# Two decoder blocks on one core: token tiles put in order of precedence at the layer boundaries, boundary weights split on VectorE, recurrence constants computed earlier

## The chip, the cores and the metric

The kernel runs on one core of a Trainium2 chip. The metric is the device time of one execution in microseconds. Engines: TensorE (PE; PEld are its weight loads), VectorE (DVE), ScalarE (ACT), GpSimd (POOL) and SyncE (SP, whose queue issues most DMAs).

## The reference

512 tokens of width 1024 in float32 go through a first block of two layers and then a second block with its own mixers and a feed-forward part. Only what lies around the change is cut out here:

```python
h = _layernorm(x, ln_in_g, ln_in_b)
for layer in range(2):
    proj = jnp.einsum('bsd,de->bse', h, w_in[layer])     # 13 segments: aq ak av ag bq bk bv bf bg cq ck cv cg
    ...                                                  # three attentions, gated: ya, yb, yc
    y = jnp.einsum('bse,ed->bsd', jnp.concatenate([ya, yb, yc], -1), w_out[layer])
    h = _layernorm(sqrt(2) * h + y, ln_g[layer], ln_b[layer])   # DEEPNORM_ALPHA = 4 ** 0.25
# second block
p_lb = softmax(hgrn_lb_logits, axis=0); lower_bounds = cumsum(p_lb, axis=0) - p_lb[0:1]
h = rms_norm(x, attn_norm); proj = h @ w_in              # bi, iw, bf, ... are segments of it
...
log_f = logaddexp(log(max(lb, 1e-30)), log1p(-lb) + log_sigmoid(f_raw)); k_in = (1 - lb) * sigmoid(-f_raw)
```

Every norm works on one token at a time, over its 1024 values.

## The kernel before

**Tiling.** The tokens are four tiles of 128 (NT = 4), one token per partition. A projection needs the normed tokens transposed, features on the partitions, and nearly in full float32 precision: both operands are held as a rounded part (hi) and a residual (lo), and mm3 (lines 193 to 199) makes three matmuls of each product: hi·hi, hi·lo, lo·hi. For the tokens this split is made by split_half (253): four transposes on TensorE into PSUM, a cast to hi on ScalarE (262), the residual on VectorE (263, tile hTl). For the weights it is made by weights (167): a DMA on SP's queue into wraw, a cast on ScalarE (189, whi), a subtraction (190, wlo). The subtraction is VectorE's, except where the caller gives another engine: the weights at the start and at the ends of the two layers (lines 343, 345, 367, 1060, 1061) give GpSimd. There are two buffers of whi and two of wlo.

**A layer's end** (layer1, 555 to 610). most (564) adds six of the eight parts of the output projection to the residual tiles res, in four column blocks c of 256 and in each over the four tiles t; line 576 is the addition on VectorE. Then rest(t) (590) adds the last two parts for a tile: two halves of six matmuls of 512 columns, each added on VectorE with a sum for the mean (598). norm(t) (601) is the layer norm (272): line 276 the mean, 278 a pass on ScalarE for the sum of squares, 279 and rsqrt (217; 221, 241, 245: seven dependent operations on one column), 286 and 287 gain and bias on each half, then a store of the tile on SP's queue (603). After the first layer split_x follows and values' step (347), which projects the tile (two groups of 24 matmuls); after the second the rms norm of the second block (post_rms, 857: squares on ScalarE, rsqrt, scaling in line 847), its transposes, and begin2's step (1063), again two groups of 24.

**The order of the work.** A scheduler fixes the order of every engine when the program is built. An instruction's place is its position in the program, less the offset of an enclosing high_priority; as the engines come free in the builder's reckoning, each takes the ready instruction with the lowest place. HP is 3000. The attention parts run with an offset of HP (ahead, 132). pipe (289) writes the stages for the tiles skewed, stage 0 of tile t beside stage 1 of tile t - 1, without any offset, and rest is called for all four tiles before it:

```python
for t in range(NT):
    rest(t)
self.pipe(*tail)          # tail: norm, the post stages, the next stage's projection
```

**The start** (355). Tile 0 of x is loaded, then the first weights; norm(t) loads the tiles 1 to 3 itself (378). Gain and bias rows are made by 32 small matmuls (373).

**The constants.** Hgrn's constructor (1522), at the start of the second block, computes the lower bounds and their logarithms: two DMAs on ScalarE's queue, eight operations on 1 to 8 columns on VectorE and three activations (1529 to 1543).

Of the kernel before, what the change touches and what calls it, by code (L numbers as in the profile page):

```python
# [13 lines left out]
AF = mybir.ActivationFunctionType  # L14
ALU = mybir.AluOpType
# [4 lines left out]
P = 128  # L20
S = 512
NT = S // P
D = 1024
KD = D // P
# [4 lines left out]
HP = 3000  # L29
# [4 lines left out]
class Net:  # L34
    def __init__(self, ctx, tc, a, out):
        self.ctx, self.tc, self.nc, self.a, self.out = ctx, tc, tc.nc, a, out
        pool = lambda name, bufs=1, **k: ctx.enter_context(tc.tile_pool(name=name, bufs=bufs, **k))
        self.cp = pool("const")
        self.sb = pool("sb")
        self.pool = None  # L40
        self.ps = pool("ps", space=PSUM)
        self.dr = pool("dr", space=DRAM)
        self.n = 0
        self.setup()

    def nm(self, s):
# [117 lines left out]
        self.sel = sel  # L164


    def weights(self, parts, n, kt=KD, eng=None):

        nc = self.nc

        def flat(tag, bufs, dt=F32, k=kt):
            m = 1056 if dt == F32 else 2112
            return self.t(tag, [P, m], bufs, dt)[:, :k * n].rearrange("p (k n) -> p k n", k=k)

        hi, lo = flat("whi", 2, F32R), flat("wlo", 2, F32R)
        kh = kt // 2 if kt % 2 == 0 else kt
        while kh * n > 1056:
            kh = (kh + 1) // 2
        parts = parts if isinstance(parts, list) else [(0, 0, parts)]
        for ka in range(0, kt, kh):  # L180
            kb = min(ka + kh, kt)
            raw = flat("wraw", 3, F32, kb - ka)
            for k0, c0, src in parts:
                k1, nn = k0 + src.shape[0] // P, src.shape[1]
                x, y = max(k0, ka), min(k1, kb)
                if x < y:
                    nc.sync.dma_start(raw[:, x - ka:y - ka, c0:c0 + nn],
                                      src[(x - k0) * P:(y - k0) * P].rearrange("(k p) n -> p k n", p=P))
            nc.scalar.copy(hi[:, ka:kb], raw)  # L189
            (eng or nc.vector).tensor_sub(lo[:, ka:kb], raw, hi[:, ka:kb])  # L190
        return hi, lo

    def mm3(self, out, wh, wl, xh, xl, nk, start=True, stop=True):
# [92 lines left out]
            nc.vector.scalar_tensor_tensor(y, y, mv[:, 2:3], g[half], op0=ALU.add, op1=ALU.mult)  # L286
            nc.vector.scalar_tensor_tensor(y, y, mv[:, 5:6], b[half], op0=ALU.mult, op1=ALU.add)

    @staticmethod
    def pipe(*stages):  # L290

        for t in range(NT + len(stages) - 1):
            for s, f in enumerate(stages):
                if 0 <= t - s < NT:
                    f(t - s)

    def new_hT(self):
        return (self.t("hTh", [P, KD, S], 1, F32R), self.t("hTl", [P, KD, S], 1, F32R))
# [37 lines left out]
    def values(self, l, hT, w=None):  # L336


        nc = self.nc
        v = [self.u("v", [P, D], NT) for _ in range(NT)]  # L340
        lf = self.u("lf", [P, NT, 16], 1)
        self.vl = v, lf
        w = w or self.weights(self.src1(l, "bv", 0, 260), 260, eng=nc.gpsimd)
        if l:
            wc = self.weights(self.src1(l, "cv"), 256, eng=nc.gpsimd)

        def step(t):
            ps = self.proj_n(w, 260, hT, t)
            nc.scalar.copy(v[t][:, 512:768], ps[:, 0:256])
            nc.vector.tensor_add(lf[:, t, 0:4], ps[:, 256:260], self.bfb[:, l, :])  # L350
            if l:
                nc.scalar.copy(v[t][:, 768:1024], self.proj_n(wc, 256, hT, t))
        return step

    def start(self, hT):

        nc, a = self.nc, self.a
        xs = [self.tk() for _ in range(NT)]

        def load(t):  # L360
            nc.sync.dma_start(xs[t], a["x"][0, t * P:(t + 1) * P, :])

        gb = self.tok.tile([16, P], F32, name="gb8", tag="gb8")
        for j, name in enumerate(("ln_in_g", "ln_in_b")):
            nc.scalar.dma_start(gb[8 * j:8 * j + 8], a[name].rearrange("(k n) -> k n", k=8))
        load(0)
        first = self.weights(self.src1(0, "bv", 0, 260), 260, eng=nc.gpsimd)
        self.bfb = self.c("bfb", [P, 2, 4])

        g, b = ([self.p(tag) for tag in tags] for tags in (("s", "s"), ("pv", "s")))  # L370
        for j, r in enumerate((g, b)):
            for k in range(8):
                nc.tensor.matmul(r[k // 4][:, k % 4 * P:k % 4 * P + P], lhsT=self.ident[:16, 8 * j + k:8 * j + k + 1].broadcast_to([16, P]),
                                 rhs=gb, start=True, stop=True)

        def norm(t):
            if t:
                load(t)
            if t == 1:
                nc.sync.dma_start(self.bfb, a["b_forget"].rearrange("(o l) h -> o l h", o=1).broadcast_to([P, 2, 4]))  # L380
            st = self.ln_stats()
            halves = [xs[t][:, :S], xs[t][:, S:]]
            if t:
                for j, x in enumerate(halves):
                    nc.scalar.activation(self.wa([P, S], BF16), x, AF.Identity, accum_out=st[:, j:j + 1])
            else:
                bs = self.tok.tile([P, 2, 6], F32, name="ln_b", tag="ln_b")
                for j, x in enumerate(halves):
                    nc.vector.bn_stats(bs[:, j], x)
                nc.vector.bn_aggr(st[:, 0:2], bs)  # L390
            self.layernorm(xs[t], g, b, 1e-5, st, sums=t > 0)
            nc.gpsimd.dma_start(self.hres[:, t, :], xs[t])

        self.pipe(norm, lambda t: self.split_x(hT, t, xs[t], ("tr", "tr")), self.values(0, hT, first))

    def small1(self, pool):

# [49 lines left out]
    def layer1(self, l, hT, post, nxt):  # L447


        nc, a = self.nc, self.a  # L450
# [71 lines left out]
        scale = 64 ** -0.5  # L522
        rb, rc, ra, rg = RATES[:4]
        with self.tp(f"att{l}", "right") as self.sub:
# [30 lines left out]
            with self.tp(f"bnd{l}", "right") as self.tok:  # L555
# [48 lines left out]

                sts = {}
                tail = [norm] + [lambda t, f=f: f(t, res[t]) for f in post] + [nxt()]
                for t in range(NT):
                    rest(t)
                self.pipe(*tail)
                left.close()  # L610

    def out_tokens(self, W, xh, xl, order, evac):
# [59 lines left out]
    def att_b(self, bq, bk, v, lf, out, slot):  # L672
# [6 lines left out]
        nc.scalar.activation(e, e, AF.Ln, bias=1.0)  # L679
        nc.vector.scalar_tensor_tensor(x, x, 0.0, e, op0=ALU.min, op1=ALU.subtract)  # L680
        nc.vector.tensor_copy(lf[:, :, 4:8], x)
        nc.vector.tensor_copy(lf[:, :, 8:16], lf[:, :, 0:8])
        cumr = self.wa()
        nc.gpsimd.memset(cumr, 1.0)
# [365 lines left out]
    def begin2(self, hT):  # L1050

        self.ph1.close()
        self.phase = self.ctx2.enter_context(self.tp("ph2", "left"))
        self.ph2i = self.ctx2.enter_context(ExitStack())
        pool = self.ph2i.enter_context(self.tp("ph2i", "left"))
        self.nslot, self.na, self.npw = 24, 4, 3
        self.bi = pool.tile([P, NT, S], F32, name="bi", tag="bi")
        self.iw = self.u("iw", [P, NT, 8], 1)
        pool = self.nc.gpsimd
        ws = [self.weights(self.col2("bi", 0, 256), 256, eng=pool),  # L1060
              self.weights([(0, 0, self.col2("bi", 256, 256)), (0, 256, self.col2("iw", 0, 8))], 264, eng=pool)]

        def step(t):
            self.nc.scalar.copy(self.bi[:, t, 0:256], self.proj_n(ws[0], 256, hT, t))
            ps = self.proj_n(ws[1], 264, hT, t)
            self.nc.scalar.copy(self.bi[:, t, 256:512], ps[:, :256])
            self.nc.scalar.mul(self.iw[:, t, :], ps[:, 256:264], (64 ** -0.5) * (8 ** -0.5))
        return step
# [450 lines left out]
class Hgrn:  # L1519


    def __init__(self, net, hT, col):
        self.net, self.nc, self.hT, self.col = net, net.nc, hT, col
        nc, a = net.nc, net.a
        s = lambda tag, n: net.u(tag, [P, n], 1)

        lg, e, den, lb, la, l1, kc, gb = (s(t, n) for t, n in (("hlg", 4), ("hle", 4), ("hld", 4), ("hlb", 4),
                                                                ("hla", 4), ("hl1", 4), ("hkc", 8), ("hgb", 1)))
        nc.scalar.dma_start(lg, a["hgrn_lb_logits_2"][0].rearrange("(h p) -> p h", p=P))
        nc.vector.tensor_sub(e, lg, lg)  # L1530
        nc.scalar.activation(e, e, AF.Exp)
        nc.vector.reciprocal(den, e)
        nc.vector.tensor_mul(e, e, den)
        nc.vector.tensor_sub(lb, e, e)
        nc.vector.tensor_scalar_max(la, lb, 1e-30)
        nc.scalar.activation(la, la, AF.Ln)
        nc.scalar.activation(l1, lb, AF.Ln, scale=-1.0, bias=1.0)
        nc.vector.tensor_scalar(kc[:, 0:4], lb, -0.5, 0.5, op0=ALU.mult, op1=ALU.add)
        nc.vector.tensor_scalar(kc[:, 4:8], lb, 0.5, -0.5, op0=ALU.mult, op1=ALU.add)
        nc.scalar.dma_start(gb, a["hgrn_out_norm_2"][0].rearrange("(p o) -> p o", o=1))  # L1540

        nc.vector.tensor_scalar_mul(gb, gb, 0.25)
        self.la, self.l1, self.kc, self.gb = la, l1, kc, gb
        self.lev = net.sub.tile([P, 9, P], F32R, name="lev", tag="lev")
        nc.gpsimd.dma_start(self.lev, a["c_lev"])
        self.lmask = net.sub.tile([P, 8, P], BF16, name="lmask", tag="lmask")
# [231 lines left out]
```

## Time and profile before

| | |
|---|---|
| median of 3 runs | 1684.64 us (1684.13 to 1685.22) |
| the profiled execution | 1684.35 us, its span 1682.6 us |
| TensorE busy | 1619.7 us (96%), 9320 matmuls |
| VectorE busy | 1067.2 us (63%), 2355 instructions |
| ScalarE busy | 730.1 us (43%), 1484 instructions |
| GpSimd busy | 129.2 us (8%), 139 instructions |

The span runs from the first to the last instruction of one execution; the time has a little around it. Busy shares are means over the span. A timeline row gives the start and the duration in us, the engine, the line of the program, the operation, what it writes and reads, its shape, and in brackets how long the engine stood idle before it and which instruction ended that. Matmuls overlap, so their spacing and not their duration is what one costs.

### The profile page before, as it was taken

How to read it: one execution, taken by the hardware profiler on the slowest of the kernel's cores; microseconds unless marked ns; L12 is line 12 of the kernel's file. 1: busy time of each engine (PE TensorE's matmuls, PEld its weight loads, DVE VectorE, ACT ScalarE, POOL GpSimd, SP SyncE). 2: the span in 40 equal slices, each digit the busy share in tenths (PEclk: the TensorE clock that was granted, in tenths of full speed). 3: DMA queues.
4: the chain of work that ended last, by engine and by line, in shares of the span. 5: the costliest groups of instructions: out<-in, count | busy, mean ns of one | idle time of the engine just before them, and what ended most of it. 6: DMA issues, size and time to landing. Idle time of an engine off the chain costs nothing.

```text
span 1682.6 us, 24320 instructions
## 1 busy us (share of the span) xinstructions
PE 1619.7 (96%) x9320; PEld 1377.5 (82%) x9320; DVE 1067.2 (63%) x2355; ACT 730.1 (43%) x1484; POOL 129.2 (8%) x139
## 2 busy tenths in 40 slices
PE   7999999989999999799889999999999999999997
PEld 6778797987777889688768876788889988888997
DVE  7686779774578796846999995624355543443233
ACT  4455654334465553465443764522233322222222
POOL 2021000020000001101321000200000000000000
PEclk9999999989999999899999999999999999999999
DMA  7453031332121413332002320233433533333321
GB/s 234 148 175 97 26 114 62 106 120 76 51 76 42 144 57 107 112 105 83 26 14 65 92 75 14 88 106 92 159 110 110 175 100 100 100 100 93 95 91 61
DMA packets 141883, 160.06 MB, mean 95 GB/s; under 512 B 14100, under 2 KB 131108, under 8 KB 141256
## 3 DMA queue, kind: packets, MB, share of 16 engines
q1 hardware_dynamic: 135960, 141.34, 27.9%
q0 software_dynamic: 2944, 11.86, 2.0%
q10 hardware_dynamic: 2864, 5.32, 1.0%
q8 instruction: 73, 1.20, 0.3%
q14 instruction: 42, 0.34, 0.1%
HBM read 143.55 MB, written 15.21 MB: 94 GB/s over the span
## 4 chain that ended last, share of the span: by engine, by line
PE 78%; DVE 13%; ACT 2%; issue 2%; DMA 1%; POOL 0%; ACTq 0%; POOLq 0%
PE pj L198 19%; PE pj L197 19%; PE pj L199 19%; PE pv L1026 3%; PE s L199 2%; PE s L197 2%; PE s L198 2%; PE tr L666 2%; PE s L769 1%; PE s L652 1%; PE s L653 1%; DVE ixs L1243 1%; DVE wlo L190 1%; PE pv L780 1%; DVE tok L286 1%
## 5 line engine op out<-in xcount | busy, mean ns | idle before, releaser
L197 PE MATMUL pj<-hTh,whi 128*128 128x512 f32 (+1 forms) x1136 | 440.8, 388 | 0.0
L198 PE MATMUL pj<-hTl,whi 128*128 128x512 f32 (+1 forms) x1136 | 440.4, 388 | 0.0
L199 PE MATMUL pj<-hTh,wlo 128*128 128x512 f32 (+1 forms) x1136 | 439.9, 388 | 0.4 <-DVE wlo L190 0.4
L190 DVE TENSOR_TENSOR wlo<-wraw,whi 128x1024 fp32r<-128x1024 f32 (+1 forms) x235 | 268.2, 1148 | 240.9 <-ACT whi L189 239.1
L189 ACT CAST whi<-wraw 128x1024 fp32r<-128x1024 f32 (+3 forms) x245 | 237.2, 982 | 358.5 <-PE pj L198 193.6
L197 PEld LDWEIGHTS pj<-hTh,whi 128*128 128x128 f32 x1136 | 213.7, 188 | 45.6 <-issue 6.8
L198 PEld LDWEIGHTS pj<-hTl,whi 128*128 128x128 f32 x1136 | 213.7, 188 | 43.4 <-issue 4.4
L199 PEld LDWEIGHTS pj<-hTh,wlo 128*128 128x128 f32 x1136 | 213.6, 188 | 43.2 <-issue 3.8
L199 PE MATMUL pj<-whi,hTl 128*128 128x256 f32 (+2 forms) x416 | 121.9, 294 | 1.6 <-DVE hTl L263 1.5
L197 PE MATMUL pj<-whi,hTh 128*128 128x256 f32 (+2 forms) x416 | 120.9, 292 | 0.9 <-ACT hTh L262 0.7
L198 PE MATMUL pj<-wlo,hTh 128*128 128x256 f32 (+2 forms) x416 | 120.9, 291 | 0.0
L198 PE MATMUL pj<-wlo,t2k 128*128 128x256 f32 x304 | 85.9, 282 | 0.0
L197 PE MATMUL pj<-whi,t2k 128*128 128x256 f32 x304 | 85.6, 281 | 0.0
L199 PE MATMUL pj<-whi,t2k 128*128 128x256 f32 x304 | 85.5, 281 | 0.0
L199 PEld LDWEIGHTS pj<-whi,hTl 128*128 128x128 f32 x416 | 81.5, 196 | 2.9 <-DVE hTl L263 2.6
L197 PEld LDWEIGHTS pj<-whi,hTh 128*128 128x128 f32 x416 | 81.9, 197 | 2.0 <-ACT hTh L262 1.7
L198 PEld LDWEIGHTS pj<-wlo,hTh 128*128 128x128 f32 x416 | 82.0, 197 | 0.5 <-DVE wlo L190 0.2
L199 PE MATMUL s<-whi,t2k 128*128 128x256 f32 x264 | 73.9, 280 | 0.0
L197 PE MATMUL s<-whi,t2k 128*128 128x256 f32 x264 | 73.9, 280 | 0.0
L198 PE MATMUL s<-wlo,t2k 128*128 128x256 f32 x264 | 73.9, 280 | 0.0
L669 ACT COPY wa<-tr 128x128 f32<-128x128 f32 (+3 forms) x96 | 40.6, 423 | 60.8 <-PE tr L666 59.5
L657 DVE CUSTOM_DVE_ANT_0 wa<-s,mask 128x128 f32<-128x128 f32 (+3 forms) x112 | 52.5, 485 | 13.4 <-PE tr L666 7.6
(440 smaller groups left out, 3056.0 us busy)
## 6 DMA issues: line engine op xcount, KB each, us to landing
wraw<-in_w_in_dram SPq DMA_DIRECT2D x112, 512.0 KB, 3.9
wraw<-in_w_ffn_gate_dram SPq DMA_DIRECT2D x22, 512.0 KB, 4.7
wraw<-in_w_ffn_up_dram SPq DMA_DIRECT2D x22, 512.0 KB, 4.8
wraw<-in_w_ffn_down_dram SPq DMA_DIRECT2D x16, 512.0 KB, 4.7
tok<-hres SPq DMA_DIRECT2D x12, 512.0 KB, 8.5
wraw<-in_w_out_dram SPq DMA_DIRECT2D x12, 512.0 KB, 3.5
hres<-tok SPq DMA_DIRECT2D x12, 512.0 KB, 3.3
wraw<-in_w_out_dram SPq DMA_DIRECT2D x8, 384.0 KB, 3.2
```

Of the source, the lines that this page charges most:

```text
L189: nc.scalar.copy(hi[:, ka:kb], raw)
L190: (eng or nc.vector).tensor_sub(lo[:, ka:kb], raw, hi[:, ka:kb])
L197: nc.tensor.matmul(out, lhsT=wh(k), rhs=xh(k), start=start and k == 0, stop=False)
L198: nc.tensor.matmul(out, lhsT=wh(k), rhs=xl(k), start=False, stop=False)
L199: nc.tensor.matmul(out, lhsT=wl(k), rhs=xh(k), start=False, stop=stop and k == nk - 1)
L286: nc.vector.scalar_tensor_tensor(y, y, mv[:, 2:3], g[half], op0=ALU.add, op1=ALU.mult)
L652: nc.tensor.matmul(sc, lhsT=stacked[:, rows], rhs=twice[hh][:, cols], start=True, stop=False)
L653: return nc.tensor.matmul(sc, lhsT=stacked[:, rows], rhs=twice[2 + hh][:, cols], start=False, stop=stop)
L657: self.nc.vector.tensor_tensor_reduce(p[:, :w], sc[:, :w], self.maskw[:, S - w:] if mask is None else mask, scale=1.0, scalar=3e38, op0=AL ...
L666: x = nc.tensor.transpose(pt[:, j, :], src[:, j * P:(j + 1) * P], self.ident)
L669: nc.scalar.copy(dst[:, :n, :], pt[:, :n, :])
L1026: x = self.nc.tensor.matmul(out, lhsT=l, rhs=r, start=k == 0, stop=k == i)
```

## The change

There are three edits. pipe now gives every stage of tile t an offset of 3000 x (5 - t) places, and rest becomes its first stage. The weights at the start and at the layers' ends are split on VectorE. The recurrence constants move from Hgrn's constructor into att_b, which runs first in layer one, and into the pool of constants.

```diff
-    def weights(self, parts, n, kt=KD, eng=None):
+    def weights(self, parts, n, kt=KD):
...
-            (eng or nc.vector).tensor_sub(lo[:, ka:kb], raw, hi[:, ka:kb])
+            nc.vector.tensor_sub(lo[:, ka:kb], raw, hi[:, ka:kb])
...
-    @staticmethod
-    def pipe(*stages):
+    def pipe(self, *stages):
         for t in range(NT + len(stages) - 1):
             for s, f in enumerate(stages):
                 if 0 <= t - s < NT:
-                    f(t - s)
+                    with self.tc.high_priority(HP + HP * (NT - t + s)):
+                        f(t - s)
...
-        w = w or self.weights(self.src1(l, "bv", 0, 260), 260, eng=nc.gpsimd)
+        w = w or self.weights(self.src1(l, "bv", 0, 260), 260)
...
-                for t in range(NT):
-                    rest(t)
-                self.pipe(*tail)
+                self.pipe(rest, *tail)
...
         nc.vector.tensor_copy(lf[:, :, 4:8], x)
+        if not self.bounds:
+            self.hgrn_bounds()
         nc.vector.tensor_copy(lf[:, :, 8:16], lf[:, :, 0:8])
```

hgrn_bounds holds the lines 1525 to 1543 as they were, with its tiles from the pool of constants, and sets self.bounds, which Hgrn's constructor reads. The same edit as in values stands in lines 345, 367, 1060 and 1061.

## Rows read from the trace of the kernel before

**Rows 1.** Busy time of each engine in two stretches, PE clock, DMA share, GB/s.
```profile
core 0: us, PE busy (x) PEld busy (x) DVE busy (x) ACT busy (x) POOL busy (x), PEclk, DMA share, GB/s
350.00:360.00 10.00, 4.83 (x22) 3.77 (x21) 10.00 (x23) 4.54 (x8) 6.20 (x4) 0.70 0.35 105
680.00:690.00 10.00, 0.00 (x0) 0.00 (x0) 9.79 (x26) 4.55 (x12) 5.89 (x4) 0.58 0.68 203
```

**Rows 2.** Timeline of PE, end of the first layer.
```profile
340.12 0.40 PE L197 MATMUL pj<-whi,ox 128*128 128x512 f32 x1
...
350.89 0.40 PE L199 MATMUL pj<-whi,ox 128*128 128x512 f32 x1
...
359.06 0.59 PE L199 MATMUL pj<-whi,hTl 128*128 128x260 f32 x1 [1.52 <-DVE hTl L263]
...
364.21 0.29 PE L197 MATMUL pj<-whi,hTh 128*128 128x256 f32 x1
...
383.86 0.28 PE L197 MATMUL pj<-whi,hTh 128*128 128x256 f32 x1
...
386.74 0.40 PE L197 MATMUL pj<-hTh,whi 128*128 128x512 f32 x1
```

**Rows 3.** Timeline of PE, end of the second layer.
```profile
666.56 0.40 PE L197 MATMUL pj<-whi,ox 128*128 128x512 f32 x1
...
690.21 1.09 PE L258 MATMUL tr<-ident,wa 128*128 128x128 f32 x4 [12.49 <-DVE wa L847]
...
720.05 0.40 PE L197 MATMUL pj<-hTh,whi 128*128 128x512 f32 x1
```

**Rows 4.** Timeline of DVE, end of the first layer.
```profile
334.48 1.22 DVE L190 TENSOR_TENSOR wlo<-wraw,whi 128x1024 fp32r<-128x1024 f32 x1
...
340.32 0.42 DVE L576 SCALAR_TENSOR_TENSOR tok<-tok,pj 128x256 f32<-128x256 f32 x1 [1.69 <-PE pj L199]
...
353.13 2.38 DVE L287 SCALAR_TENSOR_TENSOR tok<-tok,ln_st,ln_b 128x512 f32<-128x512 f32 x1
...
355.49 2.78 DVE L286 SCALAR_TENSOR_TENSOR tok<-tok,ln_st,ln_g 128x512 f32<-128x512 f32 x1
...
368.04 0.74 DVE L286 SCALAR_TENSOR_TENSOR tok<-tok,ln_st,ln_g 128x512 f32<-128x512 f32 x1
...
376.23 0.68 DVE L263 TENSOR_TENSOR hTl<-s,hTh 128x512 fp32r<-128x512 f32 x1
```

**Rows 5.** Timeline of POOL: start, end of the first and of the second layer.
```profile
7.07 4.72 POOL L190 TENSOR_TENSOR wlo<-wraw,whi 128x1040 fp32r<-128x1040 f32 x2 [3.98 <-ACT whi L189]
...
352.61 5.12 POOL L190 TENSOR_TENSOR wlo<-wraw,whi 128x1024 fp32r<-128x1024 f32 x2 [6.22 <-ACT whi L189]
...
679.59 5.23 POOL L190 TENSOR_TENSOR wlo<-wraw,whi 128x1056 fp32r<-128x1056 f32 x2 [6.84 <-ACT whi L189]
```

**Rows 6.** Timeline of DVE, end of the second layer.
```profile
671.51 1.26 DVE L1530 TENSOR_TENSOR hle<-hlg 128x4 f32<-128x4 f32 x1
...
679.75 2.80 DVE L287 SCALAR_TENSOR_TENSOR tok<-tok,ln_st,ln_b 128x512 f32<-128x512 f32 x1
...
682.54 2.83 DVE L286 SCALAR_TENSOR_TENSOR tok<-tok,ln_st,ln_g 128x512 f32<-128x512 f32 x1
...
712.40 0.69 DVE L263 TENSOR_TENSOR hTl<-s,hTh 128x512 fp32r<-128x512 f32 x1
```

**Rows 7.** Timeline of DVE, the start.
```profile
4.40 1.29 DVE L389 BATCH_NORM_STATS2 ln_b<-tok 128x6 f32<-128x512 f32 x2 [4.40 <-DMA tok<-in_x_dram]
...
6.60 0.16 DVE L245 SCALAR_TENSOR_TENSOR rs_i<-rs_t,rs_i 128x1 f32<-128x1 f32 x1
...
7.24 2.23 DVE L241 SCALAR_TENSOR_TENSOR rs_t<-rs_i,ln_st 128x1 f32<-128x1 f32 x1
...
9.50 2.31 DVE L245 SCALAR_TENSOR_TENSOR ln_st<-rs_t,rs_i 128x1 f32<-128x1 f32 x1
...
37.08 0.67 DVE L263 TENSOR_TENSOR hTl<-tr,hTh 128x512 fp32r<-128x512 f32 x1
```

**Rows 8.** Timeline of ACT, the start.
```profile
9.28 0.63 ACT L385 ACTIVATE wa<-tok 128x512 bf16<-128x512 f32 x1 [0.18 <-DMA tok<-in_x_dram]
```

More of the change, by code (lines that the diff above doesn't have):

```diff
@@ L43, in __init__ @@
         self.n = 0
+        self.bounds = None
         self.setup()
@@ L342, in values @@
         self.vl = v, lf
-        w = w or self.weights(self.src1(l, "bv", 0, 260), 260, eng=nc.gpsimd)
+        w = w or self.weights(self.src1(l, "bv", 0, 260), 260)
         if l:
-            wc = self.weights(self.src1(l, "cv"), 256, eng=nc.gpsimd)
+            wc = self.weights(self.src1(l, "cv"), 256)
         def step(t):
@@ L366, in start @@
         load(0)
-        first = self.weights(self.src1(0, "bv", 0, 260), 260, eng=nc.gpsimd)
+        first = self.weights(self.src1(0, "bv", 0, 260), 260)
         self.bfb = self.c("bfb", [P, 2, 4])
@@ L394, in start, with hgrn_bounds @@
         self.pipe(norm, lambda t: self.split_x(hT, t, xs[t], ("tr", "tr")), self.values(0, hT, first))
+    def hgrn_bounds(self):
+        nc, a = self.nc, self.a
+        s = lambda tag, n: self.c(tag, [P, n])
+        lg, e, den, lb, la, l1, kc, gb = (s(t, n) for t, n in (("hlg", 4), ("hle", 4), ("hld", 4), ("hlb", 4),
+                                                                ("hla", 4), ("hl1", 4), ("hkc", 8), ("hgb", 1)))
+        nc.scalar.dma_start(lg, a["hgrn_lb_logits_2"][0].rearrange("(h p) -> p h", p=P))
+        nc.vector.tensor_sub(e, lg, lg)
+        nc.scalar.activation(e, e, AF.Exp)
+        nc.vector.reciprocal(den, e)
+        nc.vector.tensor_mul(e, e, den)
+        nc.vector.tensor_sub(lb, e, e)
+        nc.vector.tensor_scalar_max(la, lb, 1e-30)
+        nc.scalar.activation(la, la, AF.Ln)
+        nc.scalar.activation(l1, lb, AF.Ln, scale=-1.0, bias=1.0)
+        nc.vector.tensor_scalar(kc[:, 0:4], lb, -0.5, 0.5, op0=ALU.mult, op1=ALU.add)
+        nc.vector.tensor_scalar(kc[:, 4:8], lb, 0.5, -0.5, op0=ALU.mult, op1=ALU.add)
+        nc.scalar.dma_start(gb, a["hgrn_out_norm_2"][0].rearrange("(p o) -> p o", o=1))
+        nc.vector.tensor_scalar_mul(gb, gb, 0.25)
+        self.bounds = la, l1, kc, gb
     def small1(self, pool):
@@ L1058, in begin2 @@
         self.iw = self.u("iw", [P, NT, 8], 1)
-        pool = self.nc.gpsimd
-        ws = [self.weights(self.col2("bi", 0, 256), 256, eng=pool),
-              self.weights([(0, 0, self.col2("bi", 256, 256)), (0, 256, self.col2("iw", 0, 8))], 264, eng=pool)]
+        ws = [self.weights(self.col2("bi", 0, 256), 256),
+              self.weights([(0, 0, self.col2("bi", 256, 256)), (0, 256, self.col2("iw", 0, 8))], 264)]
         def step(t):
@@ L1524, in __init__ @@
         nc, a = net.nc, net.a
[L1525 to L1543, printed above, removed]
+        self.la, self.l1, self.kc, self.gb = net.bounds
         self.lev = net.sub.tile([P, 9, P], F32R, name="lev", tag="lev")
```

## The prediction

> **What bounds the kernel now.** I read the shares of each engine first: TensorE is busy for nearly the whole span, so only a stretch in which it stands still can give much. The table by stretches finds two. In 350 to 360 us it is busy for 4.83 of 10 us, in 680 to 690 for none, while VectorE is busy for 10.00 and 9.79 [rows 1]. These are the ends of the two layers, where the changed code stands, so VectorE's chain is what ends last there.
>
> The timeline of TensorE gives the size. At the first layer's end the twelve matmuls of each token tile's last output part (function rest) run from 340.12 to 351.3; the projections of the next stage get going at 359.06 and the next stage proper starts at 386.74 [rows 2]. The 23 matmuls from 359.06 to 364.21 are spaced 0.22 us, against 0.12 for the 24 from 383.86 to 386.74 [rows 2]: the lower of its two levels (1.2 against 2.4 GHz), after a stretch whose mean granted clock was 0.70 [rows 1]. At the second layer's end the same work starts at 666.56, the first transposes come at 690.21 after 12.49 us of waiting for VectorE, and the stage ends at 720.05 [rows 3].
>
> VectorE's timeline says why. The additions of tiles 1 to 3 stand among the steps of tile 0's norm, and some steps are far longer than their like: 2.38 and 2.78 us, where the same shape takes 0.74 at 368.04 [rows 4]. They lie inside GpSimd's weight split, 352.61 to 357.7 [rows 5]; 2.80 and 2.83 at the second end lie against the one from 679.59 to 684.8 [rows 5, 6]; so do 2.23 and 2.31 at the start, beside 0.16 for the same kind just before [rows 5, 7].
>
> **The change, part by part.** The order of each engine is fixed when the program is built: of what is expected to be ready, the lowest place goes first. The change moves the stages of tile t down by 3000 times (5 - t) places, rest among them.
>
> *Splits to VectorE.* One half-weight split costs 1.22 us there [rows 4], two are a weight. Four are added at each layer's end (4.9 us) and two at the start (2.4 us). What GpSimd's reads held up comes back: 2.38 + 2.78 - 2 x 0.74 = 3.7 us at the first end [rows 4], 2.80 + 2.83 - 2 x 0.74 = 4.15 at the second [rows 6], 2.23 + 2.31 - 2 x 0.2 = 4.1 at the start [rows 7]. So this part nearly pays for itself and gains little alone. The Trainium skill (Perfetto Trace Analysis, Optimizing Scalar/DVE Operations) would rather take work off a saturated VectorE, though it warns that sending it to GpSimd may not help because the two share a read port; by its first half the 4.9 us would be pure loss, and that is a rival below.
>
> *Tile-first order.* Today rest follows all of the earlier output parts; its weights are split by about 335.7 [rows 4], yet the last of those parts is added only at 340.32 (1.69 idle + 0.42 busy = 2.11 us per tile, [rows 4]). With the lower place rest of tiles 0 and 1 can go ahead of the last two of these, so VectorE starts on tile 0 some 2 x 2.11 = 4.2 us sooner. Upper bound: all that is before 340.32; lower: nothing, should the weights be late by the builder's reckoning. I take 4.2, since the weights are there. Within the chain, tile 0's steps no longer stand behind the additions of tiles 1 to 3; that changes which tile is first, not VectorE's total. Transposes, casts and matmuls are the same in number. rest(2) and rest(3) then hold two of three PSUM buffers until the late parts are added; the third lets these through, so I add nothing.
>
> Queues: a norm's store to the residual goes through SP's queue, where loads of later weights stand behind it; it comes no later than now, so 0; were it to hold them, the weights' 1.22 us split times two would be late next. The gain's load (ScalarE's queue) and the bias load (SP's) also move forward; nobody waits for them today.
>
> At the start tiles 1 to 3 now load inside the moved stages, but tile 0 and the first weights do not: SP issues three tiles of 512 KB ahead of them. The first load is there at 4.40, the fourth at 9.28 [rows 7, 8], so tile 0 and the weights come 4.9 us later and tile 1 takes the first place. All four tiles need the gain and bias rows from TensorE anyway, and VectorE has the same work in another order, so I take 0 with a loss of 4.9 as the bound.
>
> *Recurrence constants.* The first of eight small VectorE steps took 1.26 us in the worst place [rows 6]; I count that one off and leave out the seven others. In layer one they run beside projections that keep TensorE busy: 0, and at most those 1.26 us if the first attention chain waits for them.
>
> **The sum.** At each end VectorE is the limit, so I move the end of its last residual split and let TensorE finish the last tile: two groups of 24 matmuls, each 386.74 - 383.86 = 2.88 us [rows 2], so 5.8.
> First end: 376.23 + 0.68 = 376.9 [rows 4]; - 4.2 - 3.7 + 4.9 = 373.9; + 5.8 = 379.7 against 386.74: **7.0 us**.
> Second end: 712.40 + 0.69 = 713.1 [rows 6]; - 4.2 - 4.15 - 1.26 + 4.9 = 708.4; + 5.8 = 714.2 against 720.05: **5.9 us**.
> Start: 37.08 + 0.67 = 37.75 [rows 7]; - 4.1 + 2.4 = 36.05: **1.7 us**, at which everything behind it starts earlier.
> Together 14.6. The profiled execution took 1684.35 us (span 1682.6, 1.75 around it), 0.29 under the median of 1684.64; 1684.35 - 14.6 = 1669.8, and I say **1670**. A difference of 0.2% (3.4 us) is what a measurement here can tell from none.
>
> **The rivals.**
> *A, TensorE never waits.* VectorE's idle time shrinks and TensorE alone limits: from 340.12, 11.2 us of rest and four tiles of 5.8 make 374.4, and the transposes of four tiles come on top (eight groups of at most 1 us as at 690.21 [rows 3]): 382 at worst, 374 at best. Both ends together would give up to 12 + 19, but the second has more work per tile on VectorE; I set 23 us in all: 1661. For it: 9.79 of 10 busy is work that could have started earlier. Against: VectorE's work doesn't shrink.
>
> *B, rest is not moved forward.* The weights count as ready too late, and the 4.2 us fall away twice: 14.6 - 8.4 = 6.2, so 1678. For it: the second half of the split ends less than 5 us before the last addition [rows 4].
>
> *C, nothing comes back for the splits.* The long steps were held by something else, and the 3.7, 4.15 and 4.1 us stay: 14.6 - 12 = 2.6, so 1682, no change that can be told. This is where the first half of the rule that the Trainium skill gives (same page and section) leads. Against: every long step lies inside a split of GpSimd [rows 4 to 7].
>
> *D, slower: the splits starve.* The new weights keep their ordinary place, now behind every step of every tile, and VectorE is full. If a split waits until all four chains are done, the four tiles' matmuls (4 x 5.8 = 23 us) come after it: 373.9 + 23 = 396.9 against 386.74 and 708.4 + 23 = 731.4 against 720.05, so 10.2 + 11.4 = 21.6 us lost, 1706. It decides from the point where the last split comes later than 386.7 - 23 = 363.7 in the first end or 720.05 - 23 = 697 in the second. For it: 10.00 and 9.79 busy of 10 [rows 1]. Against: the constants' first step, which stands behind the norms in the program, got in at 671.51 amid tile 0's chain [rows 6]; while one step waits for the one before it, a ready one of any place is let in.
>
> **How the numbers follow.** Forecast 0.52 (own range 1664 to 1676), A 0.08, B 0.18, C 0.09, D 0.13. The range takes the forecast, A's near side, B and C's near side, 1660 to 1682: below it lies part of A, above it D and part of C. Its bounds also hold the late loads at the start (4.9 us) and the constants' 1.26. Faster by over 0.2% (under 1681.3): forecast, A and B, 0.78. Within: C, 0.09. Slower: D, 0.13.
>
> **What would show it.** In the changed profile GpSimd has no split left and no step of this shape on VectorE is over 1 us; the matmuls of rest for tile 0 come before the last additions of the earlier parts; the first transposes after the second layer start before rest's last matmul or within 2 us of it, not 12.49 after; each end is 5 to 8 us shorter, and the rest of the kernel the same. Wrong if TensorE waits for a weight split (line 190's lower half) for more than a few us in either end, or if the matmuls there still run at the lower level for long after a new gap, or if the start grows by the late first tile.

## The result, and the profile after

The changed kernel is slower: 1693.63 us in the median of 5 runs (1691.89 to 1697.86) against 1684.21 of the kernel before beside it, a ratio of 1.0061 (95% interval 1.0046 to 1.0075). The forecast was 1670 and the range ended at 1682, so both the sign and the range were wrong. The profiled execution took 1693.63 us, with a span of 1691.9.

First the shares of each engine on the page of the changed kernel, then one stretch of the start, in the kernel before (first row) and in the changed one, and the two stretches of the changed kernel that answer to [rows 1] (columns: length, busy time and instructions of TensorE, its weight loads, VectorE, ScalarE and GpSimd, then granted clock, share and GB/s of the DMA engines).

```profile
PE 1618.2 (96%) x9320; PEld 1373.9 (81%) x9320; DVE 1066.8 (63%) x2365; ACT 730.7 (43%) x1484; POOL 104.5 (6%) x129
```

```profile
40.00:50.00 10.00, 10.00 (x73) 9.45 (x73) 5.40 (x15) 6.48 (x15) 0.00 (x0) 1.00 0.65 165
40.00:50.00 10.00, 6.29 (x39) 5.82 (x39) 4.45 (x19) 2.06 (x5) 0.00 (x0) 0.83 0.58 147
350.00:360.00 10.00, 10.00 (x51) 8.29 (x50) 8.28 (x27) 3.15 (x6) 0.00 (x0) 1.00 0.02 7
690.00:700.00 10.00, 0.09 (x1) 0.12 (x2) 9.86 (x34) 4.32 (x9) 0.00 (x0) 0.50 0.64 192
```

The hole of the first end is filled at that place: TensorE is busy for 10.00 of 10 us. The hole of the second end has only moved to 690 to 700, and the start has one that was not there: 6.29 us busy in 40 to 50 against 10.00 before.

Where the time went is told by four marks in TensorE's timeline: the first matmul of rest in either layer, the first matmul of the next stage proper, and the last of block 2's first projections. In kernels that move rest forward, the first matmul of rest comes before 17 of the 18 matmuls of the last part of w_out; I add those 17 x 0.118 = 2.0 us to the first column and to the middle, and take them off both ends, so that every kernel is cut at the same work.

```
kernel            start+layer 0  first end  middle  second end  behind
before                   340.1       46.6    279.8        53.7   962.4
after                    350.6       44.6    279.8        55.7   961.2
e1_const                 342.8       46.9    279.8        52.4   962.5
e2_split                 339.4       46.5    279.7        52.4   960.9
e3_order                 351.3       48.9    279.7        59.4   960.5
e4_no_const              345.0       46.1    279.6        56.1   961.4
e11_tail                 341.3       43.2    279.8        52.3   962.4
e12_ends                 341.1       46.1    280.0        55.9   961.1
e15_wfirst               345.8       45.2    279.7        51.8   961.6
e16_rest_behind          351.1       43.2    279.7        52.0   961.4
e18_rest0                339.2       42.9    279.9        50.8   961.7
```

After against before: 10.5 us are lost at the start, 2.0 gained at the first end, 2.0 lost at the second, 1.2 gained behind it; 9.3 in all, the difference of the spans. A single profile has its own spread: e2_split and e11_tail have the same start, and theirs differ by 1.9 us. So the verdicts below go by the medians of the runs, and the table says where to look.

**The start.** Timeline of the changed kernel, all engines, 0 to 18 us (start, duration, engine, line, operation, and in brackets the idle time before and what ended it; ACTq is ScalarE's queue of DMA issues).

```profile
0.81 0.47 ACTq L404 DMA_DIRECT2D hlg<-in_hgrn_lb_logits_dram  x1
1.31 0.52 ACTq L415 DMA_DIRECT2D hgb<-in_hgrn_out_norm_dram  x1
2.47 0.28 ACTq L366 DMA_DIRECT2D gb<-in_ln_in_b_dram  x1
...
6.86 0.15 DVE L417 TENSOR_SCALAR hgb<-hgb 128x1 f32<-128x1 f32 x1 [2.89 <-DMA hgb<-in_hgrn_out_norm_dram]
6.93 1.28 DVE L390 BATCH_NORM_STATS2 ln_b<-tok 128x6 f32<-128x512 f32 x2
8.65 3.75 PE L374 MATMUL s<-gb,ident 16*128 16x128 f32 x16 [8.65 <-DMA gb<-in_ln_in_b_dram]
9.70 1.28 ACT L411 ACT_TABLE_LOAD   x1
...
16.48 2.00 ACT L190 CAST whi<-wraw 128x1040 fp32r<-128x1040 f32 x2
```

The recurrence constants, called in the first layer's attention, have no input that they must wait for and a high place, so they were issued as the first work of the program. Their loads stand ahead of the norm's gain rows, which TensorE gets at 8.65 us, and VectorE's step on the second of them (hgb) waits 2.89 us for its load ahead of tile 0's statistics, which began at 4.40 before [rows 7]. Tile 0's own load did go first of the four, at 1.26. The first weights are loaded behind all four tiles, at 6.86, just after the load of hgb has landed (6.84), and cast behind the sums and squares of the other tiles' norms, at 16.48.

**The second end.** Timelines of TensorE, ScalarE and VectorE.

```profile
683.73 0.39 PE L200 MATMUL pj<-whi,ox 128*128 128x512 f32 x1
683.96 0.28 PE L199 MATMUL pj<-wlo,t2k 128*128 128x256 f32 x1
684.16 2.00 ACT L190 CAST whi<-wraw 128x1024 fp32r<-128x1024 f32 x2 [15.48 <-PE pj L200]
686.06 1.15 ACT L279 ACTIVATE wa<-tok,ln_st 128x1024 bf16<-128x1024 f32 x1
...
686.39 0.41 DVE L600 SCALAR_TENSOR_TENSOR tok<-tok,pj 128x256 f32<-128x256 f32 x1
687.85 0.15 DVE L280 TENSOR_SCALAR ln_st<-ln_st 128x1 f32<-128x1 f32 x1
...
699.91 1.09 PE L259 MATMUL tr<-ident,wa 128*128 128x128 f32 x4 [13.79 <-DVE wa L871]
```

Rest of all four tiles (operand ox, 48 matmuls from 672.96) runs between the first and the second matmul of the last part of w_out (operand t2k, going on at 683.96). Till rest is done ScalarE stands still for 15.48 us, at the cast of the next stage's first weights; tile 0's square stands behind that cast. VectorE adds the last part at 686.39, and tile 0's next step follows at 687.85. The first transposes come 27.0 us after rest's first matmul; before it was 23.7 [rows 3], against 25.0 when both are cut at the same work.

**The splits.** VectorE's groups of instructions in 350 to 400 us (busy time, mean ns of one).

```profile
L287 DVE SCALAR_TENSOR_TENSOR tok<-tok,ln_st,ln_g 128x512 f32<-128x512 f32 x8 | 5.9, 744 | 0.0
L288 DVE SCALAR_TENSOR_TENSOR tok<-tok,ln_st,ln_b 128x512 f32<-128x512 f32 x8 | 5.6, 747 | 0.1
```

The steps that took 2.38 and 2.78 us [rows 4] are gone: eight of each kind have a mean of 744 and 747 ns.

### The profile page after: what moved, and what is told of

Same layout as the page of the kernel before. It is cut to its first block, busy times and chain, and to the rows that moved or that the text cites. A ratio compares the mean times of both kernels' runs of the same rounds, so it can differ in the third digit from the quotient of the medians.

```text
span 1691.9 us, 24306 instructions
## 1 busy us (share of the span) xinstructions
PE 1618.2 (96%) x9320; PEld 1373.9 (81%) x9320; DVE 1066.8 (63%) x2365; ACT 730.7 (43%) x1484; POOL 104.5 (6%) x129
## 4 chain that ended last, share of the span: by engine, by line
PE 78%; DVE 12%; ACT 2%; issue 2%; DMA 1%; POOL 0%; ACTq 0%; POOLq 0%; DVEq 0%
PE pj L198 19%; PE pj L199 19%; PE pj L200 19%; PE pv L1050 3%; PE s L199 2%; PE s L198 2%; PE s L200 2%; PE tr L688 2%; PE s L674 1%; DVE wlo L191 1%; PE s L793 1%; PE s L675 1%; DVE ixs L1266 1%; ACT whi L190 1%; PE s L1326 1%
## 5 line engine op out<-in xcount | busy, mean ns | idle before, releaser
L191 DVE TENSOR_TENSOR wlo<-wraw,whi 128x1024 fp32r<-128x1024 f32 (+3 forms) x245 | 281.8, 1156 | 244.6 <-ACT whi L190 240.7
```

The costliest lines, as they stand in the source:

```text
L191: nc.vector.tensor_sub(lo[:, ka:kb], raw, hi[:, ka:kb])
```

## The experiments

**One edit at a time: e1_const, e2_split, e3_order, e4_no_const.** e1 has only the move of the constants, e2 only the splits, e3 only the places, each as in the change; e4 is the change without the constants' move.

```diff
 e1: + if not self.bounds: self.hgrn_bounds()
 e2: - w = w or self.weights(self.src1(l, "bv", 0, 260), 260, eng=nc.gpsimd)
     + w = w or self.weights(self.src1(l, "bv", 0, 260), 260)
 e3: + with self.tc.high_priority(HP + HP * (NT - t + s)):
     + self.pipe(rest, *tail)
```

> The kernel before with the recurrence constants alone moved. Theory 1 (they have no input to wait for and a high place, so they are issued at the very start of the program and hold up the first tile and the first weights there): the start grows by the 2.5 to 3.5 us by which the first statistics and the norm's gains came later in the changed kernel, block 2 gives back 1.3, so 1686 to 1687. If the constants carry the whole 8.5 us of the start: 1691 to 1692. Rival (they lie beside other work, as predicted): 1683 to 1685.

> The kernel before with the weight splits of the start and the two ends on VectorE, nothing else. Theory (the hold-ups of VectorE's long steps really go, 3.7 to 4.15 us at each of three places, and the splits' own 2.4 to 4.9 us come in their stead): within 3 us of before, 1681 to 1688. Rival (the splits stand in the chain of the tiles and are what made the changed kernel slower): 1690 or more. Rival (the hold-ups were the whole cost and the splits lie beside): 1673.

> The kernel before with the tile-first places alone (rest as the first stage, every stage of a tile ahead of the next tile's), splits still on GpSimd, constants where they were. Theory 2 (the places at the start put three tiles' loads and lambda's Exp ahead of the first weights and of tile 3, and at the ends low-placed weight casts enter the in-order queue ahead of a chain): start 4 to 6 us longer, ends no shorter, 1686 to 1692. Rival (the places gain at the ends as predicted, 4.2 us at each, and the start is untouched): 1676 to 1680.

> The changed kernel with the recurrence constants back in block 2. Theory 1 (constants cost the start 2.5 to 3.5 us): 1691 to 1692 against 1693.6 for the whole change. If they carry the start's whole 8.5 us: 1686 to 1687. If they cost nothing: 1693.6 to 1695.

Measured: e1 1685.15 us (ratio 1.0007, 0.9998 to 1.0016), e2 1681.21 (0.9987, 0.9978 to 0.9996), e3 1701.55 (1.0109, 1.0094 to 1.0125), e4 1690.04 (1.0040, 1.0027 to 1.0054). The places alone lose 17 us, more than either side of what I expected; with the splits on VectorE beside them 11.5 of these go. The splits alone gain 3.1. The constants alone stretch the start by 2.6 and give 1.3 back at the second end, and the median lies between my two ranges; in company with the other edits they cost 3.6. So the loss sits in the places, and the constants add to it.

**Start or ends: e5_start, e6_ends, e9_sepplace.** Places at one of the two alone, splits on VectorE. The other part was written with the same block and a place of zero.

```diff
+    def pipe(self, *stages, place=HP):
+                    with self.tc.high_priority(place + place * (NT - t + s)):
 e6, e9: at the start  place=0       e5: at the ends  place=0
 e9:     rest(t) in a loop of its own ahead of self.pipe(*tail)
```

> The splits on VectorE, and the tile-first places at the start alone; both ends as before, no constants moved. Theory (three tiles' loads go ahead of the first weights there, whatever the ends do): the start up to the first residual matmul 3.5 to 4 us longer than with the splits alone (339.35), and the whole 1684.5 to 1685.5. Rival (the start grew only together with the constants): 1681 to 1682.

> The splits on VectorE, and the tile-first places with rest as first stage at the two ends alone; the start as before, no constants moved. Theory (rest of all tiles goes ahead of the last part of w_out, so a weight buffer that this part used is freed late, the first weights of block 2 are cast late, and in ScalarE's queue that cast stands ahead of tile 0's square): 1686 to 1688, the loss in the second end. Rival (the ends gain as predicted and the loss was the start's alone): 1673 to 1678.

> As the run before it in this list, but rest is left out of the places: it keeps its low place behind the last part of w_out, and only the norm, the transposes and the projections of a tile go ahead of the next tile's. Theory (it is the forward move of rest that loses): the second end back to 52 us or less, the whole 1676 to 1681. Rival (the places of norm and transposes lose by themselves): 1684 to 1688.

Measured: e5 1692.05 us (1.0041, 1.0027 to 1.0055), e6 1693.05 (1.0049, 1.0036 to 1.0063), e9 1686.36 (1.0013, 1.0004 to 1.0022). All three miss, because a place of zero is not "as before". e9's start took 349.3 us, where the same code without such a block takes 341.3 (e11_tail); e5's first end took 48.4 against 46.5 (e2) and its middle 281.9 against 279.7. The likely reason, which no run shows by itself, is that the block hands its count of places back at its end, so that what the program has behind it shares them. Only the parts with a real place can be read: e5's start is 344.5, 5.2 longer than e2's, and e9's first end is 43.2.

**The ends alone, rightly: e11_tail, e12_ends, e13_tail_late, e14_behind, and the constants late: e10_late.** The start is the plain loop of before. e11 gives norm, transposes and projections of a tile their places and leaves rest behind the last part of w_out; e12 gives rest its place too, as the change does. e14 is e12 with the first casts of block 2 ordered behind tile 0's square; for that these weights are asked for inside the step of tile 0, which gives their loads, casts and splits its place too. e10 is e2, e13 is e11, with the constants tied behind the softplus of the second layer (e10 and e13 issue their first load at 385.0 and 383.1 us); the change calls them in the first layer.

```diff
 e11: +                for t in range(NT):
      +                    rest(t)
      +                self.pipe(*tail)
 e12: +                self.pipe(rest, *tail)
 e14: +            x = nc.scalar.copy(hi[:, ka:kb], raw)
      +            self.after(x, behind)
      +            if not ws:
      +                ws.append(self.weights(self.col2("bi", 0, 256), 256, behind=self.square))
 e10, e13: +        last = nc.scalar.activation(e, e, AF.Ln, bias=1.0)
           +        x = nc.scalar.dma_start(lg, ...)
           +        self.after(x, last)
```

> The splits on VectorE, and the recurrence constants in layer one but issued behind layer one's own softplus on ScalarE, so that they cannot go to the start; no tile-first places. Theory (the constants lose only because they run at the start): the start as with the splits alone (339.35), the second end 1 us shorter, 1679.5 to 1680.5. Rival (their count is on the path of layer one as well, about 1.3 us, and two more table loads): 1681.5 to 1683.

> Splits on VectorE; at the two ends norm, transposes and projections of a tile have a place ahead of the next tile's, rest keeps its low place behind the last part of w_out; the start and the constants as before (no place at all there, not a place of zero as in e9_sepplace). Theory (the places of the chain gain, the forward move of rest and the places at the start lose): start 339.3, first end 43.2, middle 279.7, second end 52, so 1675 to 1677. Rival (the short first end of e9_sepplace was bought by its long start): 1680 to 1682.

> As e11_tail, but rest is the first stage and has a place too, as in the change. Theory (rest goes ahead of the last part of w_out, the next weights' buffer comes free late, their cast stands ahead of tile 0's square): the second end 3 to 4 us longer than with the splits alone, the first end no shorter, the whole 1683 to 1686, 8 us more than e11_tail. Rival (rest's place costs nothing): as e11_tail.

> e11_tail with the recurrence constants in layer one behind its own softplus. Theory (their count is off block 2's path, and beside projections in layer one): 1 us less than e11_tail. Rival (as e10_late against e2_split, nothing gained): equal to e11_tail within 0.5 us.

> e12_ends, with the casts of block 2's first weights put behind the square of tile 0 in ScalarE's queue (an order of issue, no wait). Theory (that cast, standing ahead of the square and waiting for rest's last matmul, is what holds tile 0 at the second end): the square of tile 0 at its residual's end, some 7 us earlier than in e12_ends, the first transpose with it, the second end 3 to 6 us shorter than e12_ends. Rival (the weights' own late arrival at the projections sets the end): the second end as in e12_ends within 1 us.

Measured: e10 1681.98 us (0.9984, 0.9975 to 0.9993), e11 1679.15 (0.9968, 0.9959 to 0.9978), e12 1685.24 (1.0006, 0.9995 to 1.0016), e13 1677.68 (0.9965, 0.9952 to 0.9978), e14 1685.96 (1.0010, 1.0001 to 1.0019). Rest's place costs 6.1 us, and the intervals of e11 and e12 lie apart: shown. By the marks of one profile each, 2.9 us of the loss lie in the first end (46.1 against 43.2) and 3.6 in the second. In the first end the transposes are not late; TensorE waits four times there, 5.1 us in all, against 2.9 in e11, with the longest wait, 2.3 us, before a projection, and why was not followed. The places of the norms and transposes by themselves stand 2.1 under e2, by a first end of 43.2 instead of 46.5; the two intervals touch, and e11 lies between the two ranges I had given. The constants, moved to the second layer, are worth nothing that can be told: e10 stands 0.8 over e2, e13 1.5 under e11, within the intervals.

e14 speaks against my first account of the second end, that the cast ahead of tile 0's square is what holds it. Timeline of e14, ScalarE, VectorE and TensorE:

```profile
665.13 1.15 ACT L280 ACTIVATE wa<-tok,ln_st 128x1024 bf16<-128x1024 f32 x1 [8.22 <-DVE ln_st L278]
...
674.38 0.42 DVE L583 SCALAR_TENSOR_TENSOR tok<-tok,pj 128x256 f32<-128x256 f32 x1 [2.67 <-PE pj L201]
674.84 0.69 DVE L605 SCALAR_TENSOR_TENSOR tok<-pj,tok 128x512 f32<-128x512 f32 x1
675.46 0.15 DVE L282 TENSOR_SCALAR ln_st<-ln_st 128x1 f32<-128x1 f32 x1
...
689.05 1.09 PE L260 MATMUL tr<-ident,wa 128*128 128x128 f32 x4 [14.71 <-DVE wa L853]
```

The square now runs as soon as its sums are there, 3.9 us after rest's first matmul (661.19) where it was 13.1 in e12, and nothing comes of it: the first transposes still come 27.9 us after that matmul (27.0 in e12). Tile 0's next step stands in VectorE's queue behind the addition of the last part (L583), for which VectorE waits until TensorE has done all of rest and then the last part. Two queues held tile 0, ScalarE's until rest was done and VectorE's until the last part behind rest was done, so to free one changed nothing. That freeing both would have changed something is read from the traces and was not run by itself; e18 below shortens both waits. The rival of e14, that the weights come late to the projections, is out: TensorE waits for no weight split in this end.

**The start's loss: e15_wfirst.** Places at the start alone, and tile 0's load and the first weights put ahead of tiles 1 to 3.

```diff
+        with self.tc.high_priority(6 * HP):
+            load(0)
+        with self.tc.high_priority(5 * HP):
+            first = self.weights(self.src1(0, "bv", 0, 260), 260)
```

> Splits on VectorE, tile-first places at the start alone (both ends and the constants as before), and a place for tile 0's load and the first weights ahead of tiles 1 to 3. Theory (the start lost because three tiles' loads went ahead of the first weights on SP's queue): start up to the first residual matmul 339 to 341 us as with the splits alone, against 344.5 in e5_start, the whole 1681 to 1682.5. Rival (the places of the norms and transposes lose there by themselves): start 343 or more, the whole 1685 to 1687.

Measured: 1687.52 us (1.0021, 1.0012 to 1.0030), start 345.8: the rival, half a us over its range. The order of the loads is not what the start loses. Waits of TensorE in 0 to 70 us, e2_split and then e15 (what waited, for whom; us in total, times, longest):

```profile
PE tr L258 <- DVE tok L287: 2.6, 1, 2.6
PE tr L258 <- DVE rs_i L221: 0.9, 1, 0.9
PE pj L197 <- ACT hTh L262: 0.7, 1, 0.7
PE tr L258 <- DVE hTl L263: 0.4, 1, 0.4
```

```profile
PE pj L197 <- ACT hTh L262: 3.0, 5, 0.7
PE s L944 <- DVE rs_t L241: 2.9, 1, 2.9
PE tr L258 <- DVE tok L287: 1.8, 1, 1.8
PE pj L199 <- DVE hTl L263: 1.5, 3, 1.1
```

In the plain loop the next tile's transposes stand in the midst of a tile's 24 projection matmuls, so that ScalarE and VectorE split the halves while TensorE goes on. With the places all 24 go ahead of the next tile's first transpose, and TensorE waits at nearly every half: 3.0 + 1.5 us on the split halves against 0.7 + 0.4. A further 2.9 us it stands behind a small matmul of the bias table (L944) in its own queue. The first transposes come no later (14.67 against 14.79), so it is the order from tile to tile, not the first tile. The waits shown are 9.2 us in e15 against 4.6 in e2, most of the 6.4 by which the start grew. That the places at the start lose is shown by this run; that they lose by these hand-overs is read from the traces.

**In the change itself, and together: e16_rest_behind, e17_all, e18_rest0, e19_best.** e16 is the change with rest left behind the last part; e17 is e13 with e15's start; e18 is e11 with the rest of tile 0 alone forward (12 matmuls); e19 is e18 with the late constants.

```diff
 e18: +                    if t:
      +                        rest(t)
      +                        continue
      +                    with self.tc.high_priority(5 * HP):
      +                        rest(t)
```

> The whole change with one thing undone: rest has no place and stays behind the last part of w_out. Theory (rest's forward move costs 6 us over the two ends, as e12_ends against e11_tail): 1687 to 1688.5. Rival (with the late start and the constants it costs nothing): 1692 to 1694.

> All three edits with what the runs blame taken out: rest behind the last part of w_out, first weights ahead of tiles 1 to 3 at the start, constants in layer one behind its softplus. Theory (the tile-first places gain at the first end and nothing at the start): as e13_tail_late, 1676.5 to 1679. Rival (the places at the start gain once the weights are in front): 1673 to 1676.

> e11_tail with tile 0's rest alone (12 matmuls, 2.75 us) ahead of the last part of w_out; rest of tiles 1 to 3 stays behind it. Theory (the last part's addition on VectorE and the weight buffer that it frees are late by as much rest as stands ahead of them, and tile 0's chain stands behind both): the loss against e11_tail shrinks from 6 us with 48 matmuls to 0 to 2 us, so 1679 to 1681. Rival (any rest ahead of the last part costs its place, by the order alone): 1684 to 1686. Rival (as I predicted: a rest moved forward gains what it moves): 1675 to 1677.5.

> e18_rest0 with the recurrence constants in layer one behind its softplus: splits on VectorE, norm, transposes and projections of a tile ahead of the next tile's at the two ends, tile 0's rest alone ahead of the last part of w_out, the start untouched. Theory (what was found adds up: e13_tail_late stood 1.5 us under e11_tail): 1674.5 to 1676.5. Rival (the two gains overlap at the second end): as e18_rest0, 1676.5 to 1677.5.

Measured: e16 1689.21 us (1.0031, 1.0021 to 1.0041), 4.4 under the change, its ends 43.2 and 52.0; e17 1685.01 (1.0006, 0.9997 to 1.0015), 7.3 over e13 by its start of 346.8, a miss, which is the start's loss once more; e18 1676.45 (0.9957, 0.9944 to 0.9971); e19 1676.56 (0.9961, 0.9948 to 0.9975), no better.

e18 is the nearest to what I had predicted of the order, and its time lies in the range of that rival. Timeline of its second end:

```profile
663.82 1.15 ACT L278 ACTIVATE wa<-tok,ln_st 128x1024 bf16<-128x1024 f32 x1 [8.22 <-DVE ln_st L276]
...
664.83 0.42 DVE L580 SCALAR_TENSOR_TENSOR tok<-tok,pj 128x256 f32<-128x256 f32 x1 [1.05 <-PE pj L199]
665.17 0.15 DVE L279 TENSOR_SCALAR ln_st<-ln_st 128x1 f32<-128x1 f32 x1
...
680.86 1.08 PE L258 MATMUL tr<-ident,wa 128*128 128x128 f32 x4 [6.50 <-DVE wa L855]
```

Only 2.75 us of rest stand ahead of the last part; its addition runs at 664.83, and tile 0's step right behind it. The first transposes come 21.0 us after rest's first matmul (659.88) and TensorE waits 6.50 us for them, not 13.79. Most of that gain is there with no rest moved at all; e11, at the same place:

```profile
685.35 1.09 PE L258 MATMUL tr<-ident,wa 128*128 128x128 f32 x4 [8.31 <-DVE wa L851]
```

That is 21.1 us after rest's first matmul; cut at the same work, e18 is 2.1 us ahead of it. e18 lies 8.8 us under e12, far outside both intervals, so it is the amount of rest that goes ahead, not that it goes. Against e11 its 2.7 us less are not told apart, since the intervals overlap, so that a rest moved forward gains anything is not shown. e18 and e19 are the fastest kernels found, 0.4% under the kernel before.

## Why the prediction was wrong

The medians make a ladder from the kernel before (1684.3) to the changed one (1693.6): splits on VectorE -3.1 (e2), places of norm and transposes at the ends -2.1 (e11), rest's place +6.1 (e12), the start's places +4.8 (e4), constants +3.6 (the change). The intervals of neighbouring steps lie apart, but for two pairs: those of e2 and e11 touch, and those of e4 and the change overlap by 0.0008. Undone in the change itself, rest's place gives 4.4 back (e16).

**Splits to VectorE: right.** The hold-ups went: every such step takes 0.74 us now. The step said that they nearly pay for the added splits; alone they gained 3.1, though only 0.8 of the 1.7 forecast at the start. With the tile-first places they are worth far more, 11.5 us (e3 against e4), which no step of mine foresaw. The page that spoke against this edit (the Trainium skill, Perfetto Trace Analysis, Optimizing Scalar/DVE Operations) is half borne out: not its advice to offload a saturated VectorE, but its warning about GpSimd. What the Trainium skill says in SBUF — State Buffer, Who interferes with whom, that the two engines share a pair of ports under an exclusive lock, agrees with the 2.38 to 2.83 us that became 0.74. Rival C is out.

**Tile-first order: this step failed.** It said that "rest of tiles 0 and 1 can go ahead of the last two of these, so VectorE starts on tile 0 some 2 x 2.11 = 4.2 us sooner". At the size of e18 the idea at least does not lose. But I had given the place to four tiles and counted on two. All four went at the second end, 11.0 us of TensorE's time, in front of a last part whose addition was in VectorE's queue ahead of tile 0's chain; and in ScalarE's queue tile 0's square stood behind a cast that waited for the last matmul of rest. In place of a gain of 4.2 us at each end, the place of rest lost 6.1 us over both (e12 against e11), of which this account covers the second end. The work that was passed was not late work that nobody waited for; tile 0 itself waited for it. My upper and lower bounds, "all that is before 340.32" and "nothing", had no loss in them. The sentence that rest(2) and rest(3) cost nothing, because a third PSUM buffer lets the late parts through, looked at buffers and not at the queue.

**The start: this step failed as well.** I saw tiles 1 to 3 load ahead of tile 0 and the first weights, and took 0 with a loss of 4.9 as the bound. Tile 0's load in fact stayed first; the weights alone went behind. That the loss came at the size of the bound, 4.8, is luck, for it did not come from there: with the loads put right it stays (e15, e17). What I had put down as "the same work in another order" was the loss, as the traces read, because the old order laid one tile's splits under another's matmuls. The gain of 1.7 from the splits there was drowned.

**Recurrence constants: this step failed.** "In layer one they run beside projections" went by where the call stands. They had no input to wait for and a high place, and their loads were issued from 0.81 us on, ahead of the start's own: 3.6 us more (the change against e4) in place of 0. Tied to the second layer, they were worth nothing measurable, neither the 1.26 I counted off nor a loss.

**The rivals.** A is out, since TensorE still waits 13.79 us. D named the right sign and the wrong work: the splits did not starve TensorE, which waited 0.8 us for one in the changed kernel's first end. What starved was tile 0's chain, behind work of a lower place let into the queue ahead of it. I had used that very behaviour, a ready step of any place being let in, as an argument against D. B, rest not moved forward, I priced at a loss of 8.4 us of the gain; e16 shows that it would have been better by 4.4.

Of what I said would show it: GpSimd's splits are gone and the steps are short, as said; rest of tile 0 did come before the last addition; but the first transposes came 16.2 us after rest's last matmul and not within 2, the ends gave -2.0 and +2.0 and not 5 to 8 each, and the start grew.

What stays open: why the constants cost 3.6 us with the other edits and 0.9 alone, how rest's place loses 2.9 us in the first end, and why the places lose 17 us with the splits on GpSimd. To the first the traces have a hint: the first weights' load is issued at 1.26 us with the constants alone (e1), at 3.24 with the places and no constants (e4), and at 6.86 in the change. None was tried further.

## What to carry to other kernels

Before work is given an earlier place, ask what it passes, and whether the chain that you want to speed up waits, through an in-order queue or a buffer, for the work that was passed; move as little as opens the chain. An order that finishes one tile before the next begins can take the cover from short hand-overs between engines; here it lost 4.8 to 7.3 us at the start, while the first end was 3.3 shorter with it (e11 against e2). Work with no input to wait for runs wherever its place puts it, at the program's very start if that is high, whatever stands around its call.

## What the hardware showed that I had not expected

The same program can spread with the clock that it is granted: e12's twelve runs go from 1680.38 us at a mean granted clock of 0.994 to 1689.94 at 0.989. If the missing share is time at half speed, that is 2 x 0.005 x 1684 = 17 us more at the lower level, and half of it, 8.4, is lost if TensorE is busy in that time, near the 9.6 measured. This is an estimate, and which came first, longer waits or the lower clock, is not shown. After 13.79 us of waiting the changed kernel's stretch of 690 to 700 stands at 0.50, and its first transposes take 1.09 us for four, where four without a wait before them take 0.60 (358.61); after e11's 8.31 us they take 1.09, and after e18's 6.50 us 1.08.
